# A decoder step on one core: twelve cache gathers spread among the query tiles, with the samples' query copies on GpSimd

## The chip, the cores and the metric

The kernel runs on one core of a Trainium2 chip, as one launch. The metric is the device time of that launch in microseconds (us), the median over runs. Engines are called by the profile's names: PE is TensorE's matmul (PEld its weight load), DVE is VectorE, ACT is ScalarE, POOL is GpSimd, and SP is SyncE, which issues most transfers. POOL issues the indirect transfers of this kernel from its own queue.

## The reference

One step of a two-layer decoder for a prompt of 512 positions and, with the same weights, for 8 samples of one new position each, whose earlier keys and values lie in a paged cache. Layer 0 is a causal pooling mixer and an MLP. Layer 1 is an attention of three branches (compressed, selected, window) over keys and values that are projected once, and an MLP. The part around the change, cut:

```python
D_MODEL = 1024; SEQ = 512; DEC_BATCH = 8; DEC_SEQ = 1; PAST_LEN = 256; PAGE_SIZE = 128
N_HEADS = 16; HEAD_DIM = 64; N_KV_HEADS = 4; Q_PER_KV = 4; N_BRANCH = 3; WINDOW = 512

def _query_side(x, g, w_qg, b_gate):
    h = _rmsnorm(x, g) @ w_qg
    q = h[..., : N_HEADS * HEAD_DIM].reshape(b, t, N_HEADS, HEAD_DIM)
    gate = jax.nn.sigmoid((h[..., N_HEADS * HEAD_DIM:] + b_gate).astype(jnp.float32))
    return q, gate.reshape(b, t, N_HEADS, N_BRANCH)

# layer 1, prompt
q, gate = _query_side(xp, norm_mix[layer], w_qg[j], b_gate[j])
o = _nsa_prompt(q, gate, kc_p, vc_p, ks_p, vs_p, win_rows_p, slopes)
xp = xp + o @ w_o[j]
...
# layer 1, samples: the past rows of both cached branches come through the page table
kv_s = _shared_kv(xs, norm_kv, w_kv)
past = cache_kv_pages[page_table].reshape((dec_b, past_len) + cache_kv_pages.shape[2:])
kc_s, vc_s, ks_s, vs_s = _kv_summaries(jnp.concatenate([past, kv_rows_s], axis=1), cmp_pe, cmp_w1, cmp_w2)
win_all = jnp.concatenate([state_win.astype(xs.dtype), kv_s[:, :, 2]], axis=1)
q, gate = _query_side(xs, norm_mix[layer], w_qg[j], b_gate[j])
o = _nsa_attend(q, gate, pos_s, kc_s, vc_s, ks_s, vs_s, win_all[:, :, 0], win_all[:, :, 1], pos_w, slopes)
# inside: s = einsum(q / 8, keys) - slope * distance, a masked softmax, einsum(p, values), times the gate
```

## The kernel before

Prompt and samples go through the dense products together: a row of the stream holds 512 prompt positions and 8 samples, 520 columns, in two halves of 260. A product of float32 quality is made of three passes over a high and a low part of weight and stream (`whi`/`wlo`, `xh`/`xl`), which `split_w` (L148 on ACT, L149 on DVE) and `dense` (L161) make: one tile of 128 outputs is 8 x 3 x 2 = 48 matmuls into two banks.

The place of the change is the start of layer 1's attention. `queries(tp, gp, rstd8)` makes the query tiles, four (r = 0 to 3) for each of two groups of heads (gp = 0, 1), eight in all. For each: `dense`; `scaled` multiplies both banks by the row scale into a tile `ppT` (L908, DVE, two instructions; four buffers); then, for two halves of 64 partitions, ACT writes the high part of the prompt's queries (L1049), DVE the low part (L1050), and DVE copies the 8 samples' columns into `qall` (L1052, 64 partitions x 8 elements, 16 copies in all). `qall` is cleared by a DVE memset (L1021) and `qone` by a POOL memset (L1023).

`rows4(br, kv, c)` fetches one tile `rw` of cached rows (three buffers): for branch 0 (selected) four indirect gathers L1011 on POOL's queue, 128 rows of 1 KB each; for the window branch one plain transfer on SP. `ahead`, a list made before the query tiles, holds the first three of these tiles, 12 gathers. `attend_samples`, the samples' attention, takes them from it with `pop(0)`, transposes them (L1098) and multiplies them with `qone` (L1106); it first multiplies `qall` with the samples' compressed keys (L1080, 4 column groups for j = 0 to 3: j % 2 is the group gp of `qall`).

The order: the queries of gp 0 are traced as a whole, then the first tile of gp 1, then the first unit of the prompt's attention, which needs gp 0 alone, then the other three tiles of gp 1. A unit is, for each of 8 heads, a score product (L1226, two matmuls), the bias and row maximum (L1231) and the compressed part (L1237, into `pcs` with the maximum `csm`), then exponentials (L1254), sums and reciprocals (L1255, L1256) and a scaling by sum and gate on POOL (L1259, into `s`; the compressed part's two steps on POOL are L1191 and L1200). `values` transposes `s` (L1300) and multiplies with the values (L1273). A scheduler of the framework, which simulates the engines' times, orders each engine's instructions and sets the semaphores. `tc.issue_after(i)` tells it to queue what a block traces behind instruction `i` on that engine, for issue order only.

Of the kernel before, what the change touches and what calls it, by code (L numbers as in the profile page):

```python
# [22 lines left out]
SEQ = 512  # L23
# [79 lines left out]
def tile_step(ctx, tc, I, O):  # L103
    nc = tc.nc
    V, S, G, T = nc.vector, nc.scalar, nc.gpsimd, nc.tensor
# [435 lines left out]
    with pool("st") as st, pool("sd", side="right") as sd:  # L541
# [4 lines left out]
        for i in range(4):  # L546
            t = st.tile([P, D], F32, name=f"xt{i}")
# [35 lines left out]
        for n, tiles in ((P, (0, 1, 2, 3)), (NB, (4,))):  # L583
            for i in tiles:
                t = xt[i] if i < 4 else xs
                junk = st.tile([P, D], F32, name="junk", tag="junk", bufs=2)
                S.activation(junk[:n], t, AF.Square, accum_out=ss[:n, i : i + 1])
            c = slice(tiles[0], tiles[-1] + 1)
# [10 lines left out]
        for i in range(4):  # L599
            for hf in range(2):  # L600
                b = bank()
                for k in range(4):
                    last_ = T.transpose(b[:, k * P : (k + 1) * P], xt[i][:, (hf * 4 + k) * P : (hf * 4 + k + 1) * P], ident)
                dst = xTt[:, hf * 4 : hf * 4 + 4, i * P : (i + 1) * P]
                V.tensor_copy(dst, b.rearrange("p (k c) -> p k c", k=4))
        with tc.issue_after(last_.ins):
# [3 lines left out]
            b = bank()  # L610
# [35 lines left out]
        for gi in range(4):  # L646
            for m in range(2):
# [5 lines left out]
                g_ = gT[:, 16 + k : 17 + k]  # L653
# [16 lines left out]
        for kv in range(2):  # L670
            c = slice(16 + kv * 16, 32 + kv * 16)
# [196 lines left out]
    with ExitStack() as at_:  # L868
# [5 lines left out]
        for g in range(NG):  # L874
# [4 lines left out]
            for br in range(2):  # L879
                a, w = br * 2 * (KC[0] + SEQ), KC[br] + SEQ  # L880
# [10 lines left out]
        with pool("at1") as p1:  # L891

            opP = p1.tile([P, 2, 8, P + 2], F32, name="opP")
            with pool("at2") as p2:
                xtiles = new_x()
                xa = split_x(gT[:, 32:40], xtiles)
                r = p2.tile([P, 5], F32, name="r")
# [16 lines left out]
                for mt in range(12):  # L914
                    br, kv, gp = mt // 4, (mt // 2) % 2, mt % 2
# [6 lines left out]
                    t = p2.tile([P, TOK], F32, name="kvt", tag="kvt", bufs=2)  # L922
# [10 lines left out]
                    b = bank()  # L933
# [71 lines left out]
        def rows4(br, kv, c):  # L1005

            t = aq_.tile([P, 4, 256], F32, name="rw", tag="rw", bufs=3)
            if br == 0:
                for a2 in range(4):
                    pos = 16 + kv * 16 + c * 4 + a2  # L1010
                    G.indirect_dma_start(  # L1011
                        t[:, a2], None, cache256, bass.IndirectOffsetOnAxis(ap=idx[:, pos : pos + 1], axis=0)
                    )
            else:
                nc.sync.dma_start(t, swin[:, c * 4 : (c + 1) * 4, kv])
            return t

        ahead = [rows4(0, 0, c) for c in range(3)]

        qall = aq_.tile([P, 2, 2, 32], F32, name="qall")  # L1020
        V.memset(qall, 0.0)  # L1021
# [3 lines left out]
        def queries(tp, gp, rstd8):  # L1025

            for rp in range(2):

                def parts(raw):
                    out = []  # L1030
                    rv = raw.rearrange("p k (a c) -> p k a c", a=2)
                    for par in range(2):
                        c0 = (gp * 2 + par) * 256 + rp * P
                        out.append((rv[:, :, par], wq[:, c0 : c0 + P].rearrange("(k p) c -> p k c", p=P)))
                    return out

                raw = load_w(parts).rearrange("p k (a c) -> p k a c", a=2)
                for rr in range(2):
                    r = rp * 2 + rr
                    hi, lo = split_w(raw[:, :, :, rr * HD : (rr + 1) * HD])  # L1040
                    o = dense(hi, lo, xa)
                    t = tp.tile([P, TOK], F32, name="ppT", tag="ppT", bufs=4)
                    scaled(t, o, rstd8)
                    for par in range(2):
                        hs_ = slice(par * HD, (par + 1) * HD)
                        os_ = slice((1 - par) * HD, (2 - par) * HD)
                        q2 = qst[gp * 2 + par][r]
                        inv = 1.0 / SLOPES[(gp * 2 + par) * 4 + r]
                        S.activation(q2[hs_], t[hs_, :SEQ], AF.Copy, scale=inv)  # L1049
                        V.scalar_tensor_tensor(q2[os_], t[hs_, :SEQ], inv, f(q2[hs_]), OP.mult, OP.subtract)  # L1050
                        dst = qall[hs_, :, gp].rearrange("p a (b h) -> p h a b", b=4)[:, par * 4 + r]
                        V.tensor_copy(dst, t[hs_, SEQ:].rearrange("p (b a) -> p a b", a=2))  # L1052
                    yield

        def attend_samples(tp):
# [420 lines left out]
```

## Time and profile before

| what | us |
|---|---|
| median of 3 runs | 1179.23 |
| lowest and highest | 1177.82, 1180.8 |
| the profiled execution, its own time | 1181.33 |
| its span | 1179.6 |
| PE busy | 1138.1 (96%) |
| DVE busy | 858.2 (73%) |
| ACT busy | 596.9 (51%) |
| POOL busy | 275.9 (23%) |

The span runs from the first to the last instruction that the profiler records; the own time is 1.7 us longer. Times in the rows are microseconds from the span's start. The query tiles lie between 537 and 600 us. Mean granted TensorE clock over the span: 0.986 of full speed. A row of the timeline reads: start, duration of the merged run, engine, line, operation, output and inputs, count, and in brackets the idle time before it with what ended it ("issue": nothing that the profile shows). Merged runs of PE may overlap their neighbours by a pipeline's depth.

### The profile page before, as it was taken

To read this page: it belongs to the slowest core of one execution; us is meant where nothing else is said; L and a number is where in the kernel's file an instruction comes from. 1 tells how busy PE (TensorE), PEld (TensorE's weight loads), DVE (VectorE), ACT (ScalarE), POOL (GpSimd) and SP (SyncE) were. 2 spreads that over 40 slices of the span, in tenths; PEclk is the share of its full clock that TensorE was granted. 3 is DMA by queue.
4 is the path that set the end of the run, shared out by engine and by line. 5 is a ranking of instruction groups with operands and counts; after the bars stand their busy time and mean duration, and the time that the engine had idled before them with its cause. 6 is when DMAs were issued, how large, how long until landed. Compare 5 with 4: busy or idle time off the path is not lost.

```text
span 1179.6 us, 22983 instructions
## 1 busy us (share of the span) xinstructions
PE 1138.1 (96%) x9007; PEld 1062.0 (90%) x9007; DVE 858.2 (73%) x2026; ACT 596.9 (51%) x1320; POOL 275.9 (23%) x345
## 2 busy tenths in 40 slices
PE   6899999999999999999899999999999999999996
PEld 5899999999999898999876656699999999999996
DVE  5687776777777885495587677768866766776885
ACT  5377444444444454452366565746654444444445
POOL 2024001001101331544358544603000000000132
PEclk8899999999999999999899999999999999999998
DMA  9455334324332426443301321163333233233311
GB/s 298 155 198 180 126 110 132 99 82 134 100 125 91 144 99 214 133 108 107 84 30 46 134 70 33 37 190 127 115 108 108 75 118 113 73 108 107 101 63 73
DMA packets 93731, 134.11 MB, mean 114 GB/s; under 512 B 6024, under 2 KB 69136, under 8 KB 92719
## 3 DMA queue, kind: packets, MB, share of 16 engines
q1 hardware_dynamic: 84999, 109.11, 29.5%
q0 software_dynamic: 7872, 22.80, 6.2%
q8 instruction: 71, 1.16, 0.4%
q10 hardware_dynamic: 752, 0.74, 0.2%
q14 instruction: 37, 0.30, 0.1%
HBM read 120.02 MB, written 17.24 MB: 116 GB/s over the span
## 4 chain that ended last, share of the span: by engine, by line
PE 82%; DVE 9%; DMA 3%; issue 3%; ACT 2%; POOL 1%; SPq 0%; DVEq 0%; POOLq 0%; ACTq 0%
PE mm L191 28%; PE aux L191 27%; PE mm L161 11%; PE aux L1273 3%; PE aux L1300 3%; PE mm L1226 2%; PE aux L444 2%; DVE wlo L183 1%; DVE s L1231 1%; DMA xt<-in_x_prompt_dram 1%; DMA w<-in_cmp_w_dram 1%; DMA wraw<-in_w_up_dram 1%; PE aux L488 1%; ACT s L1254 1%; PE mm L625 1%
## 5 line engine op out<-in xcount | busy, mean ns | idle before, releaser
L191 PE MATMUL aux<-hh,whi 128*128 128x260 f32 x960 | 270.0, 283 | 1.4 <-DVE xT L783 1.4
L191 PE MATMUL aux<-hl,whi 128*128 128x260 f32 x960 | 269.7, 282 | 0.0
L191 PE MATMUL aux<-hh,wlo 128*128 128x260 f32 x960 | 267.4, 283 | 0.0
L182 ACT ACTIVATE whi<-wraw 128x512 fp32r<-128x512 f32 x227 | 133.6, 624 | 194.9 <-PE mm L191 139.8
L183 DVE TENSOR_TENSOR wlo<-wraw,whi 128x512 fp32r<-128x512 f32 x227 | 156.7, 716 | 52.4 <-ACT whi L182 47.0
L191 PEld LDWEIGHTS aux<-hh,whi 128*128 128x128 f32 x960 | 180.5, 188 | 2.3 <-DVE xT L783 1.2
L191 PEld LDWEIGHTS aux<-hl,whi 128*128 128x128 f32 x960 | 180.7, 188 | 0.5
L191 PEld LDWEIGHTS aux<-hh,wlo 128*128 128x128 f32 x960 | 179.0, 188 | 0.0
L191 PE MATMUL mm<-xh,whi 128*128 128x260 f32 x552 | 155.3, 283 | 1.5 <-ACT relu L762 1.5
L191 PE MATMUL mm<-xl,whi 128*128 128x260 f32 x552 | 155.8, 283 | 0.0
L191 PE MATMUL mm<-xh,wlo 128*128 128x260 f32 x552 | 155.4, 283 | 0.2 <-DVE wlo L183 0.2
L191 PE MATMUL mm<-first,whi 128*128 128x260 f32 x696 | 131.4, 283 | 0.2 <-ACT relu L740 0.2
L783 DVE TENSOR_TENSOR xT<-aux,xT 128x260 f32<-128x260 f32 x192 | 81.4, 424 | 54.7 <-PE aux L191 54.5
L191 PEld LDWEIGHTS mm<-first,whi 128*128 128x128 f32 x696 | 108.4, 188 | 0.9 <-ACT relu L740 0.4
L161 PE MATMUL mm<-xh,whi 128*128 128x260 f32 (+1 forms) x464 | 102.3, 288 | 3.8 <-issue 2.5
L191 PEld LDWEIGHTS mm<-xh,whi 128*128 128x128 f32 x552 | 103.7, 188 | 2.1 <-ACT relu L762 1.7
L191 PEld LDWEIGHTS mm<-xh,wlo 128*128 128x128 f32 x552 | 103.7, 188 | 0.6 <-DVE wlo L183 0.4
L191 PEld LDWEIGHTS mm<-xl,whi 128*128 128x128 f32 x552 | 103.9, 188 | 0.3
L161 PE MATMUL mm<-xl,whi 128*128 128x260 f32 (+1 forms) x464 | 102.7, 289 | 0.8 <-issue 0.8
L161 PE MATMUL mm<-xh,wlo 128*128 128x260 f32 (+1 forms) x464 | 101.7, 288 | 0.8 <-issue 0.8
L191 PE MATMUL mm<-first,wlo 128*128 128x260 f32 x348 | 98.9, 284 | 0.2 <-DVE wlo L183 0.2
L182 ACT ACTIVATE whi<-wsum 128x512 fp32r<-128x512 f32 x116 | 69.6, 622 | 40.4 <-PE mm L191 29.8
(351 smaller groups left out, 2403.8 us busy)
## 6 DMA issues: line engine op xcount, KB each, us to landing
wraw<-in_w_up_dram SPq DMA_DIRECT2D x32, 1024.0 KB, 5.5
wraw<-in_w_down_dram SPq DMA_DIRECT2D x32, 1024.0 KB, 5.1
wraw<-in_w_kv_dram SPq DMA_DIRECT2D x6, 1024.0 KB, 6.1
xd<-xT SPq DMA_DIRECT2D x4, 1040.0 KB, 4.6
sq<-xd POOLq DMA_DIRECT2D x16, 260.0 KB
xr<-xd POOLq DMA_DIRECT2D x16, 260.0 KB
w<-in_cmp_w_dram POOLq DMA_DIRECT2D x32, 128.0 KB
wraw<-in_w_qg_dram SPq DMA_DIRECT2D x8, 512.0 KB, 5.6
```

Source lines behind the costliest of these rows:

```text
L161: T.matmul(o[n][:m, :HN], w[:, kt, :m], x[:, n * HN : (n + 1) * HN], start=(i == 0 and pi == 0), stop=(i == len(kts) - 1 and pi == 2),)
L182: S.activation(hi, raw_ap, AF.Copy)
L183: V.tensor_tensor(lo, raw_ap, f(hi), OP.subtract)
L191: T.matmul(o, w_[:, kt], x_[kt][:, xs], start=(start and kt == 0 and pi == 0), stop=(kt == HK - 1 and pi == 2), skip_group_check=True,)
L444: T.matmul(acc[kv], w_[:, kv, b2], o_[:, b2 : b2 + 512], start=(t == 0 and i == 0 and b2 == 0), stop=(t == 7 and i == 2 and b2 == 1),)
L488: T.matmul(acc[:, kv * PW : (kv + 1) * PW], w1[:, kv, b2], opP[:, kv, t, b2 : b2 + PW], start=(t == 0 and kv == 0 and b2 == 0), stop=(t == ...
L625: last_ = T.matmul(bs[kk][:, i * P : i * P + w], xt[i][:, k * P : (k + 1) * P], bands[i][:, k // 2, :w], start=(i == 0), stop=(i == 3), sk ...
L783: V.tensor_tensor(y[:, hn], o, y[:, hn], OP.add)
L1226: T.matmul(b[:, : k1 - k0], qs[r][:, qt * P : (qt + 1) * P], ks[br][i][:, k0:k1], start=(i == 0), stop=(i == 1),)
L1231: V.tensor_tensor_reduce(s[:, cuts[c] : cuts[c + 1]], b[:, n0 : k1 - k0], dist[:, 384 - qt * P + cuts[c] : 384 - qt * P + cuts[c + 1]], sc ...
L1273: T.matmul(o[par * HD : (par + 1) * HD], lhsT(par), pTs[par], start=start, stop=stop, skip_group_check=True,)
L1300: T.transpose(b[:, r * P : (r + 1) * P], sts[par][r][:, kt * P : (kt + 1) * P], ident)
```

## The change

The list `ahead` starts empty. Within the queries of gp 0, behind each of the tiles r = 0, 1 and 2, the four gathers of one `rw` tile are traced and queued on POOL behind the last of that tile's two copies. The 16 copies of the samples' columns into `qall` are made by POOL in place of DVE. Nothing else changes. Lines behind the change stand four further down (L1080 becomes L1084, L1226 L1230, L1259 L1263, L1300 L1304).

```diff
@@ -1015,7 +1015,7 @@
-        ahead = [rows4(0, 0, c) for c in range(3)]
+        ahead = []
@@ -1049,7 +1049,11 @@
                         dst = qall[hs_, :, gp].rearrange("p a (b h) -> p h a b", b=4)[:, par * 4 + r]
-                        V.tensor_copy(dst, t[hs_, SEQ:].rearrange("p (b a) -> p a b", a=2))
+                        g_ = G.tensor_copy(dst, t[hs_, SEQ:].rearrange("p (b a) -> p a b", a=2))
+
+                    if gp == 0 and r < 3:
+                        with tc.issue_after(g_.ins):
+                            ahead.append(rows4(0, 0, r))
                     yield
```

On POOL before, from the last of the four small transfers that spread the gates of the samples (`gS`) to the first scaling of the prompt's scores. `DMASW` names the semaphores that POOL's own transfers raise when they have landed, `DMAHW` those of other queues; a row gives waits that the instruction itself carries:

```order
L995 DMA gS_5371<-gs8_6521 32x1x3 x3
L1011 DMA rw_6550<-in_cache_kv_pages_dram,idx_80 128x256 [waits DMASW5_49,DMASW0_49,DMASW7_49,PE_49,Pool_49]
L1011 DMA rw_6550<-in_cache_kv_pages_dram,idx_80 128x256 [waits DMASW6_49]
L1011 DMA rw_6550<-in_cache_kv_pages_dram,idx_80 128x256 x2
L1011 DMA rw_6555<-in_cache_kv_pages_dram,idx_80 128x256 [waits DMASW1_49]
...
L1011 DMA rw_6560<-in_cache_kv_pages_dram,idx_80 128x256 [waits DMAHW4_49,DMASW5_49]
...
L1023 MEMSET qone_6567 128x512
L1191 TENSOR_TENSOR pcs_6577<-pcs_6577,csm_6908 128x256 [waits DMAHW3_49,DMAHW2_49,DMAHW5_49,DMAHW1_49,DMAHW6_49,DMAHW0_49,DMAHW7_49,DVE_49,Activation_49]
```

On POOL in the changed kernel, the same stretch:

```order
L1023 MEMSET qone_6552 128x512 [waits DMASW0_49,DMASW7_49,PE_49,Pool_49]
L1052 COPY qall_6550<-ppT_6625 64x2x4 [waits DVE_49]
L1052 COPY qall_6550<-ppT_6625 64x2x4 [waits Pool_49]
L1011 DMA rw_6634<-in_cache_kv_pages_dram,idx_80 128x256 [waits DMASW4_49,DMASW3_49,DMASW5_49,DMASW2_49,DMAHW4_49,DMASW1_49,Pool_49]
...
L1052 COPY qall_6550<-ppT_6693 64x2x4
L1052 COPY qall_6550<-ppT_6693 64x2x4 [waits DMASW6_49,DMASW7_49,DMASW5_49,DMASW0_49]
L1011 DMA rw_6702<-in_cache_kv_pages_dram,idx_80 128x256 [waits Pool_49]
...
L1052 COPY qall_6550<-ppT_6764 64x2x4 [waits DMASW3_49,DMASW4_49,DMASW2_49,DMASW1_49]
...
L1052 COPY qall_6550<-ppT_6832 64x2x4 [waits DVE_49]
L1052 COPY qall_6550<-ppT_6832 64x2x4 [waits DMASW6_49,DMASW7_49,DMASW5_49,DMASW0_49]
L1195 TENSOR_TENSOR pcs_6562<-pcs_6562,csm_6908 128x256 [waits DMAHW2_49,DMAHW3_49,DMAHW1_49,DMAHW5_49,DMAHW0_49,DMAHW6_49,DVE_49,DMAHW7_49,Activation_49,Pool_49]
```

Behind each group of four gathers the next tile's second copy (`ppT_6693` is r = 1, `ppT_6764` r = 2, `ppT_6832` r = 3) carries a wait for those four to have landed, and the next group stands behind that copy. The clearing of `qone` has moved ahead of all of it.

On PE, where the second query group's first tile (`mm_6848`) ends and the first scores of the prompt (`qst00` to `qst03`) stand, before:

```order
L161 MATMUL mm_6849<-xh_5380,wlo_6845 128x260
L1226 MATMUL mm_6910<-kst_5363,qst00_6534 128x160 [waits DVE_49,Activation_49]
L1226 MATMUL mm_6915<-kst_5363,qst01_6535 128x160 [waits DVE_49,Activation_49]
L1080 MATMUL aux_7247<-kcS_78,qall_6565 32x128 [waits DVE_49,PE_49]
L1226 MATMUL mm_6920<-kst_5363,qst02_6536 128x160 [waits DVE_49,Activation_49]
```

and in the changed kernel:

```order
L161 MATMUL mm_6849<-xh_5380,wlo_6845 128x260
L1230 MATMUL mm_6910<-kst_5363,qst00_6534 128x160 [waits DVE_49,Activation_49]
L1230 MATMUL mm_6915<-kst_5363,qst01_6535 128x160 [waits DVE_49,Activation_49]
L1084 MATMUL aux_7247<-kcS_78,qall_6550 32x128 [waits PE_49,Pool_49]
L1230 MATMUL mm_6920<-kst_5363,qst02_6536 128x160 [waits DVE_49,Activation_49]
```

The samples' product with `qall` (the part that needs gp 0 alone) keeps its place behind the second head's scores, and waits for POOL where it waited for DVE.

Further on PE in the changed kernel, where the dense products of gp 1's tile r = 1 (`mm_6989`) end and those of r = 2 (`mm_7054`) begin; `s_6909` is the first scaled score tile:

```order
L161 MATMUL mm_6989<-xh_5380,wlo_6985 128x260
L1304 MATMUL aux_7262<-ident_69,s_6909 128x128 [waits Pool_49]
L161 MATMUL mm_7054<-xh_5380,whi_7050 128x260 [waits DVE_49,PE_49,Activation_49]
...
L1304 MATMUL aux_7262<-ident_69,s_6909 128x128 [waits Pool_49] x2
L161 MATMUL mm_7117<-xh_5380,whi_7113 128x260 [waits DVE_49,Activation_49]
L161 MATMUL mm_7117<-xl_5381,whi_7113 128x260
L1304 MATMUL aux_7262<-ident_69,s_6909 128x128 [waits Pool_49]
L161 MATMUL mm_7054<-xh_5380,wlo_7051 128x260 [waits DVE_49]
```

These four transposes of the first head's scores stood behind all eight tiles before, as `L1300 MATMUL aux_7262<-ident_69,s_6909 128x128 [waits Pool_49] x4`.

## Rows read from the trace of the kernel before

**Rows 1.** The page: busy time by engine.
```profile
PE 1138.1 (96%) x9007; PEld 1062.0 (90%) x9007; DVE 858.2 (73%) x2026; ACT 596.9 (51%) x1320; POOL 275.9 (23%) x345
```

**Rows 2.** Waits of PE: line, what ended them, us in total, times, longest.
```profile
PE mm L161 <- issue: 4.1, 6, 1.7
PE mm L161 <- DVE csm L1237: 1.0, 1, 1.0
```

**Rows 3.** Timeline of PE, 540 to 581 us.
```profile
560.24 0.40 PE L161 MATMUL mm<-xh,wlo 128*128 128x260 f32 x2 [0.79 <-issue]
562.37 0.28 PE L161 MATMUL mm<-xh,whi 128*128 128x260 f32 x1 [1.72 <-issue]
564.53 0.58 PE L161 MATMUL mm<-xl,whi 128*128 128x260 f32 x1 [0.34 <-issue]
...
570.53 0.40 PE L161 MATMUL mm<-xh,whi 128*128 128x260 f32 x2
...
574.63 0.41 PE L1080 MATMUL aux<-kcS,qall 128*32 128x128 f32 x2
...
578.23 0.36 PE L161 MATMUL mm<-xh,whi 128*128 128x260 f32 x1 [1.03 <-DVE csm L1237]
```

**Rows 4.** Timeline of DVE, 545 to 600 us.
```profile
548.97 0.76 DVE L908 TENSOR_TENSOR ppT<-mm,ktc 128x260 f32<-128x260 f32 x2 [3.01 <-PE mm L161]
549.71 0.17 DVE L1021 MEMSET qall<- 128x128 f32 x1
...
550.86 2.84 DVE L1050 SCALAR_TENSOR_TENSOR qst<-ppT,qst 64x512 fp32r<-64x512 f32 x4
...
566.66 0.76 DVE L908 TENSOR_TENSOR ppT<-mm,ktc 128x260 f32<-128x260 f32 x2 [5.29 <-PE mm L161]
...
574.21 0.76 DVE L908 TENSOR_TENSOR ppT<-mm,ktc 128x260 f32<-128x260 f32 x2 [4.68 <-PE mm L161]
...
575.89 0.29 DVE L1231 CUSTOM_DVE_ANT_0 s<-mm,dist 128x128 f32<-128x128 f32 x1
```

**Rows 5.** Chain of waits, pieces between 537 and 612 us: start, duration, what.
```profile
578.07 0.02 DVE csm L1237
...
578.23 17.52 PE mm L161 x144
...
604.65 2.37 DMA rw<-in_cache_kv_pages_dram,idx
```

**Rows 6.** Busy time by stretch: PE, PEld, DVE, ACT, POOL, clock, DMA share, GB/s.
```profile
558.00:564.00 6.00, 2.22 (x13) 1.70 (x11) 2.57 (x6) 1.26 (x2) 4.35 (x5) 0.97 0.32 106
564.00:570.50 6.50, 6.16 (x28) 5.98 (x28) 2.48 (x6) 2.31 (x3) 0.00 (x0) 0.50 0.01 3
570.50:577.00 6.50, 6.23 (x50) 5.78 (x48) 2.77 (x21) 1.89 (x3) 0.00 (x0) 1.00 0.00 0
```

**Rows 7.** Timeline of POOL, 537 to 612 us; eight gathers like these are left out.
```profile
547.23 1.05 POOL L1011 DMA_INDIRECT rw<-in_cache_kv_pages_dram,idx  x1 [0.30 <-issue]
...
551.14 1.23 POOL L1011 DMA_INDIRECT rw<-in_cache_kv_pages_dram,idx  x1 [0.30 <-issue]
552.67 1.13 POOL L1011 DMA_INDIRECT rw<-in_cache_kv_pages_dram,idx  x1 [0.30 <-issue]
...
561.77 0.95 POOL L1011 DMA_INDIRECT rw<-in_cache_kv_pages_dram,idx  x1 [0.30 <-issue]
562.71 0.55 POOL L1023 MEMSET qone<- 128x512 f32 x1
580.89 1.47 POOL L1191 TENSOR_TENSOR pcs<-pcs,csm 128x256 f32<-128x256 f32 x1 [17.64 <-ACT s L1254]
584.55 2.20 POOL L1259 TENSOR_SCALAR s<-s,psm,gate 128x128 f32<-128x128 f32 x4 [2.19 <-DVE csm L1194]
```

**Rows 8.** The DMA queues of the whole span, that of the instructions.
```profile
q8 instruction: 71, 1.16, 0.4%
```

**Rows 9.** The copies' line: ns shortest, median, longest.
```profile
L1052 DVE COPY qall<-ppT x16: 163/172/362, 549.9 to 596.9; 64x8 f32<-64x8 f32 x16
```

## The prediction

> **What bounds the kernel now.** The page comes first: PE is busy 96% of the span [rows 1], so time can come only from the 40 us in which PE does nothing and from stretches in which its work runs slowly. The list of PE's waits says where the first kind lies. Nearly all its entries belong to other phases; one belongs to the query tiles and is odd: PE waits six times, 4.1 us in all, in L161, for nothing that the profile shows ("issue") [rows 2]. The timeline of PE puts these waits between 558 and 564.5 us [rows 3], and that of POOL shows beside them the twelve gathers of `ahead`, one after another with 0.30 us between them, from 547.23 to 562.71 us [rows 7]. PE goes on at 564.53, 2.76 us after the last gather began [rows 3, 7].
>
> What an undisturbed tile takes is read from the chain of waits: 144 matmuls, three tiles, in 17.52 us, 5.84 us each [rows 5]. The tile r = 1 was ready for DVE at 548.97 [rows 4]. Undisturbed, r = 2, r = 3 and the first tile of gp 1 would follow at 554.8, 560.7 and 566.5; r = 3 came at 566.66 and the first of gp 1 at 574.21 [rows 4]. So the place loses 6.0 us in r = 3 and 1.7 in the next tile, **7.7 us**. [...]
>
> How gathers could starve PE: the profile has a queue that carries instructions, 71 packets and 1.16 MB, 16 KB a packet [rows 8]. I read the waits as PE's next instructions standing behind the gathers' packets. The timing fits; the trace does not prove it.
>
> **The change, part by part.**
>
> *Gathers in three groups.* The rows of POOL's order show more than the diff: behind each four gathers a copy of the next tile waits until they have landed, and the next four stand behind that copy. So POOL idles between the groups, and that is where PE's instructions could come through. The expected gain is the 7.7 us, if the rest were free.
>
> *When the groups end.* The first copy needs the cleared `qall`, which DVE delivers at 549.71 + 0.17 = 549.9 [rows 4]. No row shows a copy of 64 x 8 on POOL. Its bounds: 0.17 us, DVE's median for it [rows 9], and 0.55 us, POOL's memset of 128 x 512 [rows 7]. I take 0.2, since it has only 8 elements in a row. The first gather then begins near 550.6. A gather takes 0.95 us, or 1.13 and 1.23 beside the two-input subtraction L1050 of DVE [rows 4, 7]; each is followed by 0.30 of issue, so starts lie 1.25 to 1.53 apart. From the last start of a group to its landing: 2.37 us by the chain (604.65, a later group of four) [rows 5], at most the 2.76 us after which PE went on [rows 3, 7]. So a group takes 3 x 1.25 + 2.37 = 6.1 to 3 x 1.53 + 2.76 = 7.4 us. The copy and the issue behind it add 0.5: a period of 6.6 to 7.9. I take 7.4, nearer the upper end, since each tile's subtractions fall into the group queued beside them. The third group has landed and r = 3's second copy is done at 550.6 + 3 x 7.4 - 0.3 = **572.5** (570.1 to 574.0).
>
> *The new wait.* The samples' product L1084 stands fifth among the first scores on PE and waits for that copy; PE issues in order, so everything behind it waits too: six heads' scores, and all dense tiles of gp 1 but the first. PE reaches it at 566.5 + 0.5 and would wait 5.5 us. Before, PE passed that row at 574.63 [rows 3]: the end of the stall comes 2.1 us earlier, not 7.7.
>
> *What follows.* Before, the third head's L1231 began on DVE at 575.89, its work and a weight's split ended with `csm` at 578.07, and the next dense tile began at 578.23 [rows 3 to 5]: 2.34 us. After, with two heads and the key tile's L908 done during the wait, the third head reaches DVE about 0.6 us behind L1084 (two products of 0.3), at 573.1, and the dense tile starts at 575.5; 575.7 with these products at half clock. That is **2.5 us earlier**.
>
> *The clock.* PE would stand still for 5.5 us, no less than its idle time of 3.8 us in the stretch behind which the clock fell before [rows 6]. I expect the same fall, and full clock 6.0 us after work resumes, at 578.5. Of that, 575.7 to 578.5 lies in dense work, which does half as much: **1.4 us lost**. Bounds: nothing, if the clock stays; 3.1, what the stretch at 0.50 lost before (6.5 less 3.4).
>
> *The copies leave DVE.* Sixteen of 0.17 us [rows 9]. Most lie where DVE waits for PE anyway; that of the last tile stands ahead of the copies from which the next products are fed, 0.35 us for its pair, of which I count 0.2 as **gained**. With POOL making them, L1084 is the only early reader.
>
> *The transposes moved forward.* The first head's scaled scores are now transposed at the start of gp 1's tile r = 2, and PE waits there for POOL. POOL began `pcs` at 580.89, 2.66 us behind the dense tile's start, for 1.47 us, and four scalings take 2.20 [rows 3, 7]; with the sums ready by then, as the new order of DVE has them, they end 6.3 us behind that start. PE arrives at 5.84 and needs the fourth after some six more matmuls, at 6.9. That covers it by 0.6; if the reciprocals come late, PE waits. I count **0.3 lost** (0 to 2.2, the wait for `csm` before that scaling [rows 7]).
>
> *At nothing:* the memset of `qone` (0.55) ahead of the copies, hidden while POOL waits for `qall`; SP's order, unchanged; later gathers, whose buffers and readers stand where they stood.
>
> The sum: 2.5 - 1.4 + 0.2 - 0.3 = 1.0 us gained. The profiled execution's own 1181.33 would become 1180.3. It lies 2.1 above the median of the runs, so against 1179.23 I put **1178.2**. What a measurement can tell from no change is 0.3%, 3.5 us; this is the same.
>
> [...]
>
> **The rivals.**
> - *The wait is short* (0.18). Groups at the lower bounds: the copy at 570.1, 4.5 us before 574.63, and PE stands still for only 3.1 us, so that the clock may hold. Then 2.4 us more than the forecast's 2.5 are gained, and 4.9 + 0.2 - 0.3 = 4.8: **1174.4**. For it: the row of 2.37 us. Against it: 1.13 and 1.23 beside DVE.
> - *The change does not free PE* (0.12). The groups follow each other in time after all, PE starves in them as before, and gp 1's first tile ends near 574; the copy at 572.5 is then no wait. Only the copies' 0.2 remain: **1179**. For it: only some 0.5 to 2 us of POOL between groups.
> - *The stall was the profile's* (0.14, slower). If without the recording of a profile the gathers starve PE for less, the kernel before passes its L1080 earlier, while the new wait stands in every run. Of the 7.7 us, 2.1 could be so by the difference between profiled execution and median; with 6 of them gone, PE before would pass at 568.6, 3.9 us ahead of the new 572.5; the clock's 1.4 and 0.3 come on top, less 0.2: **1184.6**. It decides from 4.1 us on, when the two kernels' gain and the clock's loss leave 3.5 us. Against it: the three runs lie within 3 us.
> - *The groups last longer* (0.08, slower). If landing behind a semaphore adds 2 us to each, the copy is done at 578.5, 3.9 behind the old passage, and with the clock 1184.5. It decides from about 577.
>
> **How the numbers follow.** The forecast has 0.48, with its own bounds from 1174.5 (groups short or the clock unharmed) to 1181.6 (copy at 574.0, clock 2.6 and more). Same: most of the forecast's chance, the second rival and some of the first, 0.58. Faster by over 3.5 us: 0.20. Slower: 0.22. The range leaves out about one in ten at either end: 1174.3 to 1184.0.
>
> **What would show it.** Right: no "issue" waits of L161 between 555 and 566; three groups of four gathers with POOL idle about 2 us behind each; PE waiting for POOL's L1052 in L1084 some 5 us until near 572.5; a second dip of the clock at 572 to 578; the next dense tile near 575.7. Wrong: issue waits of several us still there (second rival); a wait under 3 us with the clock full (first); a wait over 8 us (the fourth); the profile as forecast and a median above 1183 (the third). Wrong altogether would be a change of time that lies outside 537 to 612 us.

## The result: slower by 8 us, and the profile after

In six runs each the changed kernel took 1185.96 us (median; 1183.55 to 1187.34), the kernel before 1177.99 (1177.78 to 1180.8; the three known ahead had 1179.23): a ratio of 1.0060, 95% interval 1.0041 to 1.0080. The forecast was 1178.2, and the range ended at 1184.0.

The profiled execution of the changed kernel took 1187.13, with a span of 1185.4. That of before took 1181.33 and is not among the six timed runs; it lies 3.3 above their median.

The changed kernel's page, busy time by engine, as [rows 1]:

```profile
PE 1139.5 (96%) x9007; PEld 1063.9 (90%) x9007; DVE 854.9 (72%) x2010; ACT 596.5 (50%) x1320; POOL 277.7 (23%) x361
```

Sixteen instructions went from DVE to POOL, and nothing else in that row explains 8 us. The waits of PE between 540 and 620 us do, as [rows 2]:

```profile
PE aux L1084 <- POOL qall L1052: 7.3, 1, 7.3
PE aux L1304 <- POOL s L1263: 0.7, 1, 0.7
PE mm L161 <- DVE csm L1241: 0.3, 1, 0.3
```

The issue waits of L161 are gone; the samples' product waits 7.3 us for POOL's copies. The timeline of POOL shows why, as [rows 7]: each group's landing stands in a copy's wait.

```profile
549.02 0.55 POOL L1023 MEMSET qone<- 128x512 f32 x1
552.05 1.44 POOL L1052 COPY qall<-ppT 64x8 f32<-64x8 f32 x2 [2.48 <-DVE qall L1021]
553.77 1.30 POOL L1011 DMA_INDIRECT rw<-in_cache_kv_pages_dram,idx  x1 [0.28 <-POOL qall L1052]
...
557.91 0.94 POOL L1011 DMA_INDIRECT rw<-in_cache_kv_pages_dram,idx  x1 [0.30 <-issue]
558.90 0.19 POOL L1052 COPY qall<-ppT 64x8 f32<-64x8 f32 x1
561.08 0.19 POOL L1052 COPY qall<-ppT 64x8 f32<-64x8 f32 x1 [1.99 <-DMA rw<-in_cache_kv_pages_dram,idx]
561.54 0.96 POOL L1011 DMA_INDIRECT rw<-in_cache_kv_pages_dram,idx  x1 [0.27 <-POOL qall L1052]
...
569.18 0.97 POOL L1011 DMA_INDIRECT rw<-in_cache_kv_pages_dram,idx  x1 [0.50 <-POOL qall L1052]
...
575.88 0.68 POOL L1052 COPY qall<-ppT 64x8 f32<-64x8 f32 x3 [1.74 <-DMA rw<-in_cache_kv_pages_dram,idx]
```

The timeline of PE, as [rows 3]: four products of the first two heads, the wait, the product, and the next dense tile, at half clock (0.42 for a row that took 0.28 in [rows 3]):

```profile
568.30 0.57 PE L1230 MATMUL mm<-kst,qst 128*128 128x160 f32 x4
576.13 0.64 PE L1084 MATMUL aux<-kcS,qall 128*32 128x128 f32 x2 [7.26 <-POOL qall L1052]
576.69 2.85 PE L1230 MATMUL mm<-kst,qst 128*128 128x160 f32 x12
579.89 0.56 PE L161 MATMUL mm<-xh,whi 128*128 128x260 f32 x1 [0.34 <-DVE csm L1241]
580.24 0.42 PE L161 MATMUL mm<-xl,whi 128*128 128x260 f32 x1
```

And busy time by stretch, with the columns of [rows 6]:

```profile
558.00:564.00 6.00, 6.00 (x53) 6.00 (x52) 2.14 (x4) 1.49 (x3) 3.15 (x5) 1.00 0.21 69
564.00:570.50 6.50, 4.87 (x42) 4.71 (x40) 2.81 (x12) 2.90 (x5) 3.37 (x6) 1.00 0.20 61
570.50:577.00 6.50, 0.87 (x4) 0.49 (x4) 0.00 (x0) 0.08 (x1) 3.56 (x7) 0.61 0.24 81
577.00:586.00 9.00, 8.65 (x42) 8.47 (x41) 5.77 (x33) 5.09 (x19) 2.36 (x5) 0.52 0.61 115
586.00:600.00 14.00, 14.00 (x120) 14.00 (x119) 7.21 (x15) 3.42 (x6) 4.12 (x9) 1.00 0.40 79
```

Where before had 13 matmuls between 558 and 564, there are 53 now. The stall has moved to 569 to 576, and the half clock behind it lasts until 585.6.

Setting each matmul's start in one trace against the same one's in the other, line by line and in order, gives the account of the two profiled executions (times of before's profile). The changed kernel is 2.1 us behind at 558 us (1.5 of it from a stretch near 200 us, below). It is 5.8 ahead at 572: 7.9 gained. It is 1.5 behind at the product: 7.3 lost in the wait. It is 4.6 behind at 590: 3.1 lost at half clock. At 610 it is 3.2 behind. So from 540 to 610 us the change costs 1.1 against *this* execution of before. At their ends the two executions lie 5.8 us apart, of which 2.1 arose before the place and 1.5 at another stretch at half clock near 947 us. The place does not explain the 8 us in this pair of traces: the execution of before lies 3.3 above its timed runs, that of the changed kernel 1.2. What before does at this place in the timed runs is what the experiments had to settle.

### The profile page after: what moved, and what is told of

Its sections match the earlier page's. It is cut to its first block, busy times and chain, and to the rows that moved or that the text cites. A ratio compares the mean times of both kernels' runs of the same rounds, so it can differ in the third digit from the quotient of the medians.

```text
span 1185.4 us, 22990 instructions
## 1 busy us (share of the span) xinstructions
PE 1139.5 (96%) x9007; PEld 1063.9 (90%) x9007; DVE 854.9 (72%) x2010; ACT 596.5 (50%) x1320; POOL 277.7 (23%) x361
## 4 chain that ended last, share of the span: by engine, by line
PE 79%; DVE 9%; DMA 4%; issue 3%; POOL 3%; ACT 1%; SPq 0%; DVEq 0%; POOLq 0%; ACTq 0%
PE mm L191 27%; PE aux L191 26%; PE mm L161 9%; PE aux L1304 3%; PE aux L1277 3%; PE mm L1230 3%; DVE wlo L183 2%; PE aux L444 2%; POOL rw L1011 1%; DMA xt<-in_x_prompt_dram 1%; DMA w<-in_cmp_w_dram 1%; DMA rw<-in_cache_kv_pages_dram,idx 1%; DMA wraw<-in_w_up_dram 1%; PE aux L488 1%; DVE s L1235 1%
## 5 line engine op out<-in xcount | busy, mean ns | idle before, releaser
L161 PE MATMUL mm<-xh,whi 128*128 128x260 f32 (+1 forms) x464 | 102.8, 289 | 0.6 <-DVE csm L1241 0.3
L161 PE MATMUL mm<-xl,whi 128*128 128x260 f32 (+1 forms) x464 | 102.5, 288 | 0.0
L161 PE MATMUL mm<-xh,wlo 128*128 128x260 f32 (+1 forms) x464 | 101.7, 287 | 0.0
```

The lines of the kernel that those rows point to most:

```text
L161: T.matmul(o[n][:m, :HN], w[:, kt, :m], x[:, n * HN : (n + 1) * HN], start=(i == 0 and pi == 0), stop=(i == len(kts) - 1 and pi == 2),)
```

## Experiments

**Theory and rivals.** The theory at first, W in the expectations, was that every run of before loses the stall and that the new wait costs more. The theory that replaced it, P, is the prediction's third rival with its price corrected: the waits of L161 belong to some executions of the kernel before and not to those that were timed, so their removal was worth nothing there, while the wait for POOL is paid in full in all. The rivals: the copies on POOL or the new order of PE cost the time (run the copies on POOL without the regrouping); the time is lost far from this place, at half clock (D; look at more traces of before).

The runs came in five sets. In a set, kernels run in turn on one chip with the kernel before among them; a ratio is against the kernel before in the same set. Medians in us, the timing above as the first line:

| set | before | changed | twin | copies on POOL alone | no early gathers | groups, no landing |
|---|---|---|---|---|---|---|
| timing | 1177.99 | 1185.96 | | | | |
| 1 | 1183.60 | 1188.55 | 1179.44 | | | |
| 2 | 1178.61 | | | 1177.35 | 1177.96 | 1178.44 |
| 3 | 1183.36 | 1188.12 | 1178.05 | | 1178.74 | |
| 4 | 1178.92 | | 1178.15 | 1175.33 | | 1179.24 |
| 5 | 1184.21 | | 1180.21 | 1189.21 | | |

Sets 2 and 5 ran on the same chip, so what the expectations call a matter of the chip is one of the set.

### The kernel before, again (sets 1, 3, 4)

No edit.

> The kernel before, unchanged, profiled once more. Theory W (the stall beside the gathers belongs to every run; the change loses because PE's new wait in L1084 and the clock behind it cost as much as the stall or more): the trace shows the stall again, PE waiting about 4 us for nothing shown in L161 near 558 to 564 us and a stretch at half clock behind it, about 7.7 us lost, also where the run's own time is near 1178. Rival P (the stall of the first trace was mostly the profile's or that execution's, and a usual run has less of it): the trace shows 3 us or more less of it, with a time 3 us lower.

> The kernel before, profiled a third time, on one chip with the three that follow. Theory P (whether the gathers starve PE differs from chip to chip; both traces of before that showed it came from executions at 1181 to 1182 us): if the trace shows the issue waits of L161 (3 us or more), the twin and the kernel without gathers lie 4 us or more below; if it shows none, they lie within 1.5 us, and the time is the lower one of the two seen, near 1178. Theory W in its first form (every usual run loses the stall): the issue waits are there and the kernel without gathers is 4 to 8 us below.

> The kernel before, a fourth trace. Theory P: on a chip where its median is near 1178 the trace has no issue waits of L161 and no fall of the clock between 560 and 572; on one where it is near 1183 it has both. If the trace shows the waits also at 1178, the stall does not set the time and something else differs between the chips.

Measured: 1183.54, 1183.18 and 1178.73, each the same as the kernel before of its set (0.9997, 0.9999, 0.9997). Waits of PE, in set 1, and then in set 3:

```profile
PE mm L161 <- issue: 3.2, 5, 0.9
```

```profile
PE mm L161 <- issue: 2.5, 4, 1.1
```

In set 4 the list has no such line for L161. Busy time by stretch there, to be read against [rows 6]:

```profile
558.00:564.00 6.00, 6.00 (x52) 6.00 (x51) 2.71 (x8) 1.26 (x2) 4.48 (x6) 1.00 0.29 100
564.00:570.50 6.50, 6.50 (x55) 6.22 (x54) 3.21 (x14) 2.69 (x4) 1.94 (x3) 1.00 0.16 57
570.50:577.00 6.50, 5.20 (x28) 4.91 (x28) 6.38 (x36) 4.55 (x12) 1.04 (x1) 0.74 0.40 92
```

The same program, the same twelve gathers in one run (POOL busy 4.48 of 6.00 us, the transfers 100 GB/s, where [rows 6] have 4.35 and 106), and PE does not miss a matmul. PE passes L1080 at 569.70, 17.7 us behind the tile r = 1 on DVE, not 25.7 as in [rows 3, 4]. So the stall on which the prediction rests is there in the sets that take 1183 and absent in one that takes 1179. The 2.5 us of set 3 are less than the 3 or more that were expected. By its time of 1177.99 the timing set belongs to the sets without the stall; no trace of before was taken in it, only that of the changed kernel.

Set against this trace of set 4, the changed kernel's profile shows what the change costs where before does not stall. In times of that trace it is 0.9 ahead until 569 us, 6.7 behind at the first matmuls behind the product (7.6 lost in the wait), 8.0 behind at 590 (1.3 more at half clock) and 7.7 at 607: 8.6 lost at the place, beside the 8.0 of the timing. Before loses some time to the clock here too: in this trace it is at half from 573.5 to 576.9.

### The twin: POOL's queue as changed, the product as before (sets 1, 3, 4, 5)

The copies on POOL go into a second tile that nothing reads; DVE still fills `qall`. The order on PE, DVE (but one clearing) and ACT is that of before.

```diff
-        ahead = [rows4(0, 0, c) for c in range(3)]
+        ahead = []
+        qtwin = aq_.tile([P, 2, 2, 32], F32, name="qtwin")
+        V.memset(qtwin, 0.0)
                         V.tensor_copy(dst, t[hs_, SEQ:].rearrange("p (b a) -> p a b", a=2))
+                        twin = qtwin[hs_, :, gp].rearrange("p a (b h) -> p h a b", b=4)[:, par * 4 + r]
+                        g_ = G.tensor_copy(twin, t[hs_, SEQ:].rearrange("p (b a) -> p a b", a=2))
+                    if gp == 0 and r < 3:
+                        with tc.issue_after(g_.ins):
+                            ahead.append(rows4(0, 0, r))
```

> The changed kernel, where DVE makes the copies into qall as before, and POOL makes the same 16 copies once more into a second tile that nobody reads: POOL's queue, its waits for landed gathers and the three groups are those of the change, but the samples' product on PE waits for DVE. Theory W: PE reaches the product near 569 and passes; no wait of 7 us, no fall of the clock, no stall in L161: 8 to 10 us below the changed kernel, 1176 to 1178, or as much as 5 below before. Rival Q (the three groups themselves cost, by POOL's later work or by DMA): within 3 us of the changed kernel.

> The twin again (POOL's queue as in the change, copies into qall by DVE). Theory P: within 1.5 us of the kernel without gathers on this chip; below before by what the stall costs there. In either case 7 to 9 us below the changed kernel.

> The twin: 4 to 5 us below before where before starves, within 1.5 us of it where it does not; near 1178 on either chip.

> The twin beside it on the same chip: where the kernel before takes about 1183 us, 0.995 to 0.997 (1178 to 1179.5 us) and no issue wait of L161; where it takes about 1178 us, 0.999 to 1.001.

Measured: 0.9959 (0.9945 to 0.9974), 0.9961 (0.9945 to 0.9977), 0.9988 (0.9975 to 1.0002) and 0.9961 (0.9945 to 0.9977). Its time is 1178 to 1180 in every set, with no issue wait of L161 in any of the four traces. So parting the gathers does end the stall: it gains 4.0 to 5.3 us in the three sets at 1183 and above, and 0.8, within the interval, in set 4, where the trace of before has none. The prediction's expectation that parting ends the stall was right; its size in the runs that counted was not. Rival Q falls with it. One part of the expectation did not come: the clock falls in the twin too, in set 1 from 572.3 to 575.7, as long as in set 4's trace of before.

The changed kernel beside it:

> The changed kernel, unchanged, profiled once more. Theory W: 1184 to 1187 us again, the wait in L1084 at 7 us again, half clock for some 13 us behind it. Rival D (part of the loss is two stray stretches at half clock, near 200 and 948 us of the first trace, where PE was fully busy, 1.4 us each, and they belong to the changed program): both are there again. If they are chance, this trace has them elsewhere or not at all, and the median of the rounds still lies 6 to 8 us above before.

> The changed kernel again. Theory P: 7 to 9 us above the twin and the kernel without gathers on any chip, since PE's wait in L1084 and the half clock behind it do not depend on the stall: about 8 above before where before has no stall, about 5 where it has.

1188.55 (1.0042, 1.0029 to 1.0056) and 1188.12 (1.0033, 1.0014 to 1.0051): 9.1 and 10.1 us above the twin, which differs only in who fills the `qall` that PE reads, and in what order follows from it. Both lie above what was expected (1184 to 1187 in set 1, 7 to 9 above the twin in set 3). Set 3, PE, 545 to 612 us:

```profile
PE aux L1084 <- POOL qall L1052: 7.2, 1, 7.2
```

So where the stall exists, the change takes away some 5 us and adds 9 to 10; where it doesn't, it only adds.

### The copies on POOL alone (sets 2, 4, 5)

One line against the kernel before; the twelve gathers stay in one run. The order on PE, DVE and ACT is that of the changed kernel.

```diff
-                        V.tensor_copy(dst, t[hs_, SEQ:].rearrange("p (b a) -> p a b", a=2))
+                        G.tensor_copy(dst, t[hs_, SEQ:].rearrange("p (b a) -> p a b", a=2))
```

> The kernel before with one half of the change: POOL makes the 16 copies, the twelve gathers stay one behind another ahead of them. The order on PE, DVE and ACT is that of the changed kernel. Theory W (the loss is PE's wait in L1084 and the clock behind it): the copies are held back until the twelve have landed, near 565 us, and are done by about 567; PE, which starves in L161 as before, reaches the product near 574 and does not wait. Time within 2 us of the kernel before. Rival O (the changed order on PE, DVE and ACT costs by itself, or POOL's copies do): 4 to 6 us above before, like the changed kernel, without a wait in L1084.

> Twelve gathers one behind another, copies by POOL, the order of the change on PE, DVE and ACT (the earlier trace of it had no issue waits, on a chip where before was at 1178.6). If the gathers' train starves PE on this chip, this kernel has the waits and the time of before within 2 us. If it has no waits and lies 4 to 5 below where before has them, it is not the train of gathers as such.

> The copies on POOL without the regrouping of the gathers, once more on whatever chip comes. If the kernel before takes about 1183 us there, its dense layer waits for instructions there, and these twelve gathers stand in one run as before: theory P (the issue waits come from the gathers being issued in one run) expects them here too, 2 to 4 us of waits of L161 with no other wait, and a ratio of 0.998 to 1.000. The rival, that in this order of PE the issue waits do not arise, expects none of them and a ratio of 0.995 to 0.997. If the kernel before takes about 1178 us there, neither theory is tested: 0.997 to 1.000, no issue wait, no wait of L1084 over 1 us.

Measured: 0.9992 (0.9980 to 1.0004) in set 2 and 0.9976 (0.9957 to 0.9996) in set 4, with no wait of L1084 and no issue wait of L161. In these sets, at the level of the timing, neither the copies on POOL nor the new order costs anything, so the rival falls for the 8 us. In set 5, on the chip of set 2, the same kernel took 1189.21: 1.0042 (1.0026 to 1.0059). Waits of PE there:

```profile
PE mm L161 <- issue: 4.3, 5, 1.5
```

and by stretch:

```profile
558.00:564.00 6.00, 2.84 (x16) 2.47 (x15) 0.00 (x0) 0.00 (x0) 4.78 (x6) 0.78 0.32 109
564.00:570.50 6.50, 5.21 (x24) 5.22 (x25) 2.99 (x6) 1.42 (x3) 2.64 (x8) 0.50 0.06 21
```

The expectation of those waits held, that of the time did not: 1.0042 where 0.998 to 1.000 was expected. It is rival O's 4 to 6 us above before, without a wait in L1084, so for a set with the stall that rival is not refuted. Set against its own trace of set 4, matmul by matmul, this one is 0.4 us behind at 557 and 8.7 at 562.4, has 7.4 left at 575, and loses another 6 between 600 and 616 (times of set 4's trace); in its own time the clock is at half from 612.5 to 616.0 and from 626.2 to 629.6. Why the second place suffers too was not tried.

One program, one chip, 1177.35 and 1189.21: what makes a set have the waits is neither the program nor the chip. What it is stays open. One sign goes with it: every trace of sets 1, 3 and 5, like the profile of before on which the prediction rests, lacks records of semaphores raised by landed transfers. They hold 4164 to 4358, where the changed kernel's profile and the traces of sets 2 and 4 hold 4571 to 4573 (4379 without the early gathers). This places the timing with the sets that have no stall. It also leaves it possible that the recording itself takes part; no two runs here differ in the recording alone.

### Without the early gathers (sets 2, 3)

POOL clears the three tiles in place of the twelve gathers. The scores of three quarters of the samples' selected keys are left out, and the order of the rest is that of before.

```diff
-            if br == 0:
+            if br == 0 and kv == 0 and c < 3:
+                G.memset(t, 0.0)
+            elif br == 0:
```

> The kernel before, where the first three rw tiles are cleared by POOL in place of the twelve gathers, so that the samples' selected branch leaves out the scores of three quarters of its keys; everything else and the order on PE, DVE and ACT stay. Theory W: no issue wait of L161, no fall of the clock there: the whole stall is gained, 6 to 8 us below before. Rival P (usual runs have less of the stall than the profiled one): 3 us or less.

> As the earlier kernel without the twelve gathers: the first three rw tiles are cleared, so the scores of three quarters of the samples' selected keys are left out. Beside before on the same chip it prices the stall: theory P: 0 to 1.5 us where before's trace has no issue waits, 4 or more where it has them.

Measured: 0.9993 (0.9977 to 1.0009) in set 2 and 0.9959 (0.9948 to 0.9971) in set 3, with no issue wait of L161 in either trace. The gathers cost 4.6 us in set 3 and, within the interval, nothing in set 2.

### Groups that don't wait for their landing (sets 2, 4)

A copy of one column behind each tile on POOL anchors the next four gathers; no copy waits for a landing, and DVE fills `qall`.

```diff
-        ahead = [rows4(0, 0, c) for c in range(3)]
+        ahead = []
+        mark = aq_.tile([P, 1], F32, name="mark")
+                    if gp == 0 and r < 3:
+                        m_ = G.tensor_copy(mark, t[:, SEQ : SEQ + 1])
+                        with tc.issue_after(m_.ins):
+                            ahead.append(rows4(0, 0, r))
```

> The kernel before, where each group of four gathers is queued behind a copy of one column by POOL that waits for its query tile alone, r = 0, 1, 2, and no longer for the landing of the group before. Order on PE, DVE and ACT as before; DVE makes the copies into qall. POOL pauses for less than 1 us between groups. If a group must have landed before the next begins for PE's instructions to come through: the stall comes back in part, 0 to 3 us below before. If any pause, or the later start, is enough: as the twin, 4 to 5 us below before.

> Groups of four behind each tile without a wait for landing. On a chip where before starves: equal to the twin if any pause is enough, between before and the twin if the groups must have landed. On a chip where before does not: all within 1.5 us.

Measured: 1.0002 (0.9990 to 1.0014) and 1.0005 (0.9994 to 1.0016), no issue wait. Parting by itself is free. Both sets are ones in which the kernel before has no stall, so whether parting without a landing ends it was not seen.

### An earlier start of POOL's copies (set 2)

POOL clears `qall` itself, so that its first copy needn't wait for DVE. The order is otherwise that of the changed kernel.

```diff
-        V.memset(qall, 0.0)
+        G.memset(qall, 0.0)
```

> The changed kernel, where POOL in place of DVE clears qall, ahead of its first copy; the order of all else stays. The first group then starts when tile r = 0 is scaled, 3.5 to 4 us earlier, and so do the second and third. Theory W: PE's wait in L1084 falls from 7.2 to 3 to 4 us and the stretch at half clock gets shorter or goes; 4 to 7 us below the changed kernel, near the kernel before. Rival O: within 2 us of the changed kernel.

Measured: 1184.45, 1.0054 (1.0034 to 1.0074). Waits of PE, and POOL at the start of the place:

```profile
PE aux L1084 <- POOL qall L1052: 5.9, 1, 5.9
```

```profile
549.58 0.22 POOL L1021 MEMSET qall<- 128x128 f32 x1
549.72 0.55 POOL L1023 MEMSET qone<- 128x512 f32 x1
550.33 0.45 POOL L1052 COPY qall<-ppT 64x8 f32<-64x8 f32 x2
552.55 1.49 POOL L1011 DMA_INDIRECT rw<-in_cache_kv_pages_dram,idx  x1 [1.78 <-issue]
```

The copies are done at 550.8 and the first gather begins only at 552.55, so the wait is just 1.4 us shorter (3 to 4 us of it were expected to be left, 5.9 were), and the clock still falls (half from 572.5 to 582.7). Beside the 1178.61 of its set this is the second measurement, after the timing itself, of the wait where there is no stall to win back: 5.8 us.

### The product behind the dense tiles (set 1)

```diff
+            with tc.issue_after(last_mm[0].ins):
                 for j in range(4):
                     T.matmul(
```

(`last_mm` is the last matmul of the tile that `dense` traced last.)

> The changed kernel with one more queue edge: the samples' product L1084 stands on PE behind the last dense product of the query tiles. POOL makes the copies. Theory W: as the twin, 8 to 10 us below the changed kernel. If POOL's late scalings now hold PE up instead (they stand behind the third group's landing at 576 us), a wait of PE for POOL's s appears behind the dense products and some of it is given back. Rival Q: within 3 us of the changed kernel.

Measured: 1188.44 (1.0030, 1.0009 to 1.0051), the changed kernel's time in its set, as rival Q had it and not theory W. The total does not decide between them, for the edge moved dozens of other instructions on PE; the twin does. What this run shows is the place alone. Matmul by matmul the dense tiles run some 9 us earlier at 585 than in the changed kernel's profile, which is about the wait and the clock behind it, 7.2 + 3.0; by the end the reordered work has used all of it up (waits of L1281 for DVE of 4.7 in all up to 660 us, and three more stretches at half clock between 605 and 647).

**The other rival, D.** Stretches at half clock far from the place, with PE busy throughout, are in traces of the kernel before too: near 200 us in the three of sets 1, 3 and 4, and near 815 in that of set 4. In the changed kernel's profile they stand at 200 and 947, the first in the stretch from 198 to 204:

```profile
198.00:204.00 6.00, 6.00 (x37) 5.58 (x36) 3.37 (x13) 1.42 (x3) 0.57 (x1) 0.72 0.17 48
```

About 3.4 us at half clock, some 1.5 us lost each. Both come just behind twenty matmuls with one column (L236, 197.46 to 199.64 and 945.36 to 947.54), which in the trace of set 1 have no such stretch behind them near 200. The changed kernel's trace of set 1 has neither of the two, that of set 3 has both (200 and 951) and one more at 613. The one near 200 is no effect of the change. For the one near 947 this is not shown: a stretch between 939 and 955 stands in six of the nine traces in which a group of gathers waits for the landing of the one before (two of the changed kernel, three of the twin, the product behind the dense tiles), and in none of the other eleven. It may be 1.5 us of the loss; since the twin has it too, it is not the main part.

**A version that beats both.** The twin: 0.4% faster than before in three sets and level in the fourth. The copies on POOL alone had the lowest time of all, 1175.33 in set 4, and the highest, 1189.21 in set 5.

## Why the prediction was wrong, point by point

- *"The expected gain is the 7.7 us, if the rest were free."* This is the step that failed. The size was read rightly off the profile, and between the two profiled executions 7.9 us were gained. But the profile was of an execution 3.3 us above the median of the six timed, and a trace of before in a set at their level has no stall: PE passes L1080 there 17.7 us behind the tile r = 1, where the forecast set the new wait against a passage after 25.7. The third rival said that the timed runs might not have the stall and was given 0.14; its outcome was the case. Its reason, the recording of a profile, is not shown and stays open; the timed runs of sets 1, 3 and 5 have the higher level as well as their traces. What spoke against it, "the three runs lie within 3 us", says nothing: runs of one set agree among themselves, with the stall or without.
- *What carries the stall.* The expectation that the gathers in one run are its condition held: no trace without them has it, four with them have it, three don't. The mechanism, "PE's next instructions standing behind the gathers' packets", is not borne out. One 16 KB packet of the instruction queue falls among the gathers, from 555.50 to 556.62 in before's profile and from 558.28 to 559.33 in set 4. These are the lines of the queue in 555:557 of the first and 558:560 of the second:

```profile
q8 instruction: 1, 0.02, 3.5%
```

```profile
q8 instruction: 1, 0.02, 3.3%
```

  It took about as long where PE stalled as where it didn't, it had landed before PE's first wait (558.4), and the next comes at 581.89, long after the last. PE does not wait for a packet that the trace shows.

  More than PE's supply is late, which [rows 4] leave out. Tile r = 2 reaches DVE 9.15 us behind r = 1 in before's profile and 5.76 in set 4 (the second row; "remote" is a semaphore increment that the profile ties to no instruction):

```profile
558.12 0.43 DVE L908 TENSOR_TENSOR ppT<-mm,ktc 128x260 f32<-128x260 f32 x1 [4.42 <-remote]
```

```profile
557.74 0.76 DVE L908 TENSOR_TENSOR ppT<-mm,ktc 128x260 f32<-128x260 f32 x2 [1.05 <-PE mm L161]
```

  The tile's last three signalling matmuls begin between 554.30 and 554.54 in before's profile, ahead of any wait of PE. The semaphore increments that DVE waits for are recorded only at 557.41, 558.10 and 558.82; in set 4 each is recorded within 0.02 us of its matmul's end. The other three stalled traces have 6.9 to 14.0 us between the two tiles. So PE's signals are held up before PE itself pauses. Instructions held up behind gathers do not account for that, and what does stays open.
- *Parting the gathers.* The second rival, by which PE starves in the groups as before, fell: neither the changed kernel's profile nor the twin's four traces have an issue wait of L161, and the twin gains 4.0 to 5.3 us in three sets.
- *When the groups end.* Forecast: copy 22.8 us after DVE's clearing began (549.71 to 572.5). Measured: 24.3 (551.82 to 576.07). The two first copies took 0.71 and 0.67, not 0.2, which with the issue brings the first gather 1.1 later; the periods were 7.77 and 7.64, not 7.4, because landing took 3.17 from a group's last start (557.91 to 561.08), beyond my upper bound of 2.76.
- *The new wait.* Forecast 5.5, measured 7.26: 1.5 from the line above, and PE came 0.2 sooner. The place, the releaser and what queued behind it were as forecast.
- *The clock.* It fell as forecast, and was full again at 585.6, 9.5 us after work resumed (576.13), not 6.0 as before (564.53 to 570.53 in [rows 3]). The loss was 3.1, not 1.4, at my bound of 3.1 (28 matmuls took 6.50 us in [rows 6]; at the 17.52 for 144 of [rows 5] they take 3.4). Beside set 4's trace of before, which has 3.4 us at half clock itself, it is 1.3.
- *The dense tile 2.5 earlier.* Counted from the tile r = 1 on DVE, it began at 28.81 us (551.08 to 579.89), before at 29.26 (548.97 to 578.23): 0.45 earlier.
- *DVE's copies and the transposes.* The four moved transposes caused no wait at their new place; one of 0.7 for the scaled scores stands near 611 us. Small, as forecast.

Put together: the third rival priced PE's delay at 3.9 + 1.4. Beside set 4's trace of before it is 7.6 and 1.3, of which 0.3 is won back by 607 us; the runs show 8.0 (timing) and, beside the twin, 9.1 and 10.1. So the rival's 1184.6 was low as well, by the wait: PE came to the product 1.9 us sooner than the rival had it (17.7 and not 19.6 behind the tile r = 1), and the copies 1.5 later.

## What to carry to other kernels

A stall seen in one profiled execution is a gain only if the timed runs have it: hold that execution's time against their median, and where it lies well above, as here by 3.3 of 7.7 us, take a second trace before the stall is counted. The time alone does not tell: set 3's execution with the stall took 1180.99, 2.2 below its median, and set 4's without it 1180.01, 1.3 above. Before a copy is put behind a transfer on a queue that runs in order, as POOL's did (the copy of 561.08 waited 1.99 us for the landing, and the gather behind it began at 561.54), look for the first reader of the copy on the bound engine: here PE came to the reader 17.8 us after the tile r = 1, and the queue was done after 25.0. To have the pauses without the wait, let something that nobody reads stand behind the landings, as the twin does.

## What the runs showed of the hardware that was not expected

- *Copies on POOL beside DVE.* The first two copies took 0.71 and 0.67 us in the changed kernel, while DVE ran its two-input L1050 (552.01 to 554.85, four of 0.71); with the early clearing they ran from 550.33 to 550.78, ahead of it, at 0.2 each. Not every copy beside L1050 is slow: the one of 558.90 took 0.19 while two of L1050 ran from 558.31 to 559.72. What makes the difference was not shown.
- *The other way round, longer.* A DVE operation of 128 x 4 that elsewhere takes 0.17 took 4.46 us beside a run of eight POOL instructions (L1200, L1259, L1191) that follow each other without a gap from 617.24 to 621.63. In set 4's trace of before, DVE and then PE:

```profile
617.20 4.46 DVE L1255 TENSOR_SCALAR psm<-psm 128x4 f32<-128x4 f32 x1
```

```profile
622.19 0.61 PE L1226 MATMUL mm<-kst,qst 128*128 128x384 f32 x2 [2.74 <-DVE pmx L1231]
```

  It ended at 621.66, when POOL paused, and cost PE 2.7 us. The profile of before that the prediction rests on does not have it; it is one way in which time won at 560 us is lost at 620.
- *Two levels of one program.* The kernel before takes 1178 to 1179 us in three sets and 1183 to 1184 in three, the same chip having both, and its traces at the higher level have the waits of L161 and lack semaphore records. PE's waits end at steps of about 0.71 us there (560.24, 562.37 and 564.53 in [rows 3]), as do its late signals (558.10 and 558.82). What sets the level was not found.
